# Row softmax with temperature on one core: the code alignment directives of DVE and ACT moved from the head of the code to behind the fourth pass

## The chip, the cores and the metric

The kernel runs on one core of a Trainium2 chip. The metric is the time of one execution on the device, in microseconds (us), as the median of several runs. All runs quoted here were at a granted clock of 1.0. A "ring" below is one of the core's 16 DMA engines, seen as a serial worker: it moves one packet after the other (in the trace of the kernel before, from 60 to 280 us, all but one of the 2,909 data packets start within 8 ns of the end of another packet). The packet records do not name the ring; what is said below of single rings is worked out from the times at which packets start and end.

## The reference

```python
def setup_inputs():
    batch, seq, dim = 32, 512, 1024
    return {"x": np.random.randn(batch, seq, dim).astype(np.float32), "temperature": 0.5}

def reference(x, temperature):
    scaled = x / temperature
    shifted = scaled - np.max(scaled, axis=-1, keepdims=True)
    exp_x = np.exp(shifted)
    return (exp_x / np.sum(exp_x, axis=-1, keepdims=True)).astype(np.float32)
```

There are 16,384 rows of 1,024 floats: 67.11 MB are read once and 67.11 MB written once.

## The kernel before

The rows are cut into 16 tiles of 4 MiB (128 partitions with 8 rows each), with six buffers. A pass works on half a tile, four rows per partition; there are 32 passes. DVE takes the maxima and later scales by the reciprocal sums, ACT takes the exponentials and issues the stores, SP issues the loads.

```python
    with tc.manual_schedule():

        nc.vector.addr_align(128, offset=0, max_nops=0)
        nc.scalar.addr_align(128, offset=0, max_nops=0)
        for _ in range(BUFS):
            load()
        for g in range(len(groups) + 1):
            if g < len(groups):
                maximum(g)         # DVE: reduction, then bias
                exponential(g)     # ACT: four exponentials with sums
            if g > 0:
                divide(g - 1)      # DVE: reciprocal, then four scalings
                store(g - 1)       # ACT: after each second pass; then load() on SP
```

The two directives ask that an engine's next instruction stand at a multiple of 128 slots of its code. The trace shows one branch for each, of 33 ns on ACT (at 0.73 us) and 47 ns on DVE (at 0.76 us).

Of the kernel before, what the change touches and what calls it, by code (L numbers as in the profile page):

```python
# [1 line left out]

# [4 lines left out]



TILES = [[8]] * 16  # L10
BUFS = 6

GROUP = 4


@with_exitstack
def kernel(
    ctx: ExitStack,
    tc: tile.TileContext,
    x: bass.AP,  # L20
    temperature: bass.AP,
    out: bass.AP,
):
    nc = tc.nc
    f32 = mybir.dt.float32
    scale = 1.0 / float(temperature)
    extreme = mybir.AluOpType.max if scale > 0 else mybir.AluOpType.min

    P = 128
    xf = x.flatten_outer_dims()  # L30
    of = out.flatten_outer_dims()
    n, d = xf.shape
    assert sum(sum(ks) for ks in TILES) * P == n

    data = ctx.enter_context(tc.tile_pool(name="data", bufs=BUFS))
    stats = ctx.enter_context(tc.tile_pool(name="stats", bufs=4))


    groups, first, r = [], [], 0
    for i, ks in enumerate(TILES):  # L40
        first.append(r)
        r += sum(ks)
        a = 0
        for k in ks:
            for b in range(0, k, GROUP):
                m = min(GROUP, k - b)
                groups.append((i, a + b, m, (a, k) if b + m == k else None))
            a += k

    def dram(t, i):  # L50
        k = sum(TILES[i])
        block = t[P * first[i] : P * (first[i] + k), :]
        return block.rearrange("(p k) d -> p k d", p=P, k=k)

    tiles, small = [], []

    def load():
        i = len(tiles)
        if i < len(TILES):
            xt = data.tile([P, sum(TILES[i]), d], f32, name="xt")  # L60
            nc.sync.dma_start(out=xt, in_=dram(xf, i))
            tiles.append(xt)

    def maximum(g):
        i, a, k, _ = groups[g]
        top, bias, sums, recip = (
            stats.tile([P, k], f32, name=name) for name in ("top", "bias", "sums", "recip")
        )
        small.append((bias, sums, recip))
        nc.vector.tensor_reduce(  # L70
            out=top, in_=tiles[i][:, a : a + k, :], axis=mybir.AxisListType.X, op=extreme
        )
        nc.vector.tensor_scalar_mul(bias, in0=top, scalar1=-scale)  # L73

    def exponential(g):
        i, a, k, _ = groups[g]
        bias, sums, _ = small[g]
        for b in range(k):
            nc.scalar.activation(  # L79
                tiles[i][:, a + b, :],  # L80
                tiles[i][:, a + b, :],
                mybir.ActivationFunctionType.Exp,
                bias=bias[:, b : b + 1],
                scale=scale,
                accum_out=sums[:, b : b + 1],
            )

    def divide(g):
        i, a, k, _ = groups[g]
        _, sums, recip = small[g]  # L90
        nc.vector.reciprocal(recip, sums)  # L91
        for b in range(k):
            nc.vector.tensor_scalar_mul(  # L93
                tiles[i][:, a + b, :], in0=tiles[i][:, a + b, :], scalar1=recip[:, b : b + 1]
            )

    def store(g):
        i, _, _, part = groups[g]
        if part:
            a, k = part  # L100
            nc.scalar.dma_start(out=dram(of, i)[:, a : a + k, :], in_=tiles[i][:, a : a + k, :])
            if a + k == sum(TILES[i]):
                load()



    with tc.manual_schedule():

        nc.vector.addr_align(128, offset=0, max_nops=0)
        nc.scalar.addr_align(128, offset=0, max_nops=0)  # L110
        for _ in range(BUFS):
            load()
        for g in range(len(groups) + 1):
            if g < len(groups):
                maximum(g)
                exponential(g)
            if g > 0:
                divide(g - 1)
                store(g - 1)


# [1 line left out]
_INS = ['x', 'temperature']  # L123
_OUTS = [((32, 512, 1024), 'float32')]

_NUMBERS = {'temperature': 0.5}


# [26 lines left out]
```

## Time and profile before

| | before |
|---|---|
| time, median of 3 runs | 317.72 us (317.58 to 317.98) |
| span of the profiled execution | 315.6 us |
| busy: DVE, ACT | 75%, 47% |
| bytes moved, mean rate | 134.26 MB, 425 GB/s |
| one 32 KiB data packet on its ring (median) | 1.213 us |
| start of the first DMA packet, end of the last | 1.74 us, 314.47 us |
| code packets (8,192 B each) start at | 1.76, 3.60, 124.63, 162.34, 253.33 us |

The last three rows come from the trace's records of single DMA packets; the views of the profile only sum them up.

### The profile page before, as it was taken

Reading aid. Unit: us, or ns where it says so; the run is one execution under the profiler, and the core shown is the slowest. Engines: PE = TensorE matmul, PEld = TensorE weight load, DVE = VectorE, ACT = ScalarE, POOL = GpSimd, SP = SyncE. Lnnn points to the kernel's source line nnn. Section 1 sums busy time; section 2 is a strip of 40 time slices with the busy share of each in tenths; the row PEclk is TensorE's granted clock in tenths of the full one; section 3 lists DMA queues with packets and bytes.
Section 4 is the critical chain, followed back from the end, with each engine's and each line's share of the span. In section 5 each row is a group of like instructions: output and inputs, shape, how many; then the busy total and the mean of one; then the engine's idle time right before and its main releaser. Section 6 shows DMA issues by size and latency. Waiting matters only on the chain.

```text
span 315.6 us, 622 instructions
## 1 busy us (share of the span) xinstructions
DVE 235.5 (75%) x224; ACT 149.6 (47%) x257; POOL 0.2 (0%) x4
## 2 busy tenths in 40 slices
DVE  0299999999789494994939949498594976949720
ACT  0176666666626255361553615546065560645500
POOL 0000000000000000000000000000000000000000
DMA  8999999999999999999999999999999999999996
GB/s 330 415 448 415 386 457 407 461 411 453 424 440 432 432 432 429 444 424 453 415 454 407 457 407 457 403 461 403 461 403 461 403 462 403 461 419 444 428 436 278
DMA packets 4613, 134.26 MB, mean 425 GB/s; under 512 B 512, under 2 KB 512, under 8 KB 512
## 3 DMA queue, kind: packets, MB, share of 16 engines
q1 hardware_dynamic: 2304, 67.11, 49.7%
q10 hardware_dynamic: 2304, 67.11, 49.2%
q14 instruction: 5, 0.04, 0.0%
HBM read 67.11 MB, written 67.11 MB: 425 GB/s over the span
## 4 chain that ended last, share of the span: by engine, by line
DVE 72%; another core or an unknown queue 15%; DMA 4%; ACT 3%; issue 1%; DVEq 0%
DVE top L70 43%; DVE xt L93 27%; DMA xt<-in_x_dram 4%; ACT xt L79 3%; DVE recip L91 1%; DVE bias L73 1%; DVEq L150 0%
## 5 line engine op out<-in xcount | busy, mean ns | idle before, releaser
L79 ACT ACTIVATE xt<-xt,bias 128x1024 f32<-128x1024 f32 x128 | 145.4, 1137 | 136.0 <-DVE recip L91 118.6
L70 DVE TENSOR_REDUCE top<-xt 128x4 f32<-128x4096 f32 x32 | 141.3, 4416 | 62.2 <-DMA xt<-in_x_dram 62.2
L93 DVE TENSOR_SCALAR xt<-xt,recip 128x1024 f32<-128x1024 f32 x128 | 87.7, 749 | 1.1
L79 ACT ACTIVATION_READ_ACCUMULATOR xt<-xt,bias 128x1 f32 x128 | 23.8, 186 | 0.0
L79 ACT ACT_TABLE_LOAD x1 | 1.3, 1283 | 13.5 <-DMA xt<-in_x_dram 13.5
L91 DVE RECIPROCAL recip<-sums 128x4 f32<-128x4 f32 x32 | 5.5, 171 | 2.1 <-ACT xt L79 2.1
L73 DVE TENSOR_SCALAR bias<-top 128x4 f32<-128x4 f32 x32 | 5.5, 170 | 1.1
L136 POOL MEMSET const-bfloat16-1.0<- 128x1 bf16 x1 | 0.1, 102 | 0.0
L136 POOL MEMSET const-uint8-127<- 128x1 uint8 x1 | 0.1, 102 | 0.0
L136 POOL MEMSET const-float32-0.0<- 128x1 f32 x1 | 0.1, 99 | 0.2 <-issue 0.2
L136 POOL MEMSET const-float32-1.0<- 128x1 f32 x1 | 0.1, 99 | 0.0
## 6 DMA issues: line engine op xcount, KB each, us to landing
xt<-in_x_dram SPq DMA_DIRECT2D x16, 4096.0 KB, 50.2
out_dram<-xt ACTq DMA_DIRECT2D x16, 4096.0 KB, 38.4
```

The source lines that it names most:

```text
L70: nc.vector.tensor_reduce(out=top, in_=tiles[i][:, a : a + k, :], axis=mybir.AxisListType.X, op=extreme)
L73: nc.vector.tensor_scalar_mul(bias, in0=top, scalar1=-scale)
L79: nc.scalar.activation(tiles[i][:, a + b, :], tiles[i][:, a + b, :], mybir.ActivationFunctionType.Exp, bias=bias[:, b : b + 1], scale=scal ...
L91: nc.vector.reciprocal(recip, sums)
L93: nc.vector.tensor_scalar_mul(tiles[i][:, a + b, :], in0=tiles[i][:, a + b, :], scalar1=recip[:, b : b + 1])
L136: nc = _bacc.Bacc("TRN2", target_bir_lowering=False, num_devices=1)
```

## The change

The intent: the padding and its branch stand in the middle of the work of the second tile, not ahead of everything. Nothing else moves: the order of instructions on each engine, the loads, the stores and the waits are the same.

```diff
+ALIGNED = 3
...
     with tc.manual_schedule():
-
-        nc.vector.addr_align(128, offset=0, max_nops=0)
-        nc.scalar.addr_align(128, offset=0, max_nops=0)
         for _ in range(BUFS):
             load()
...
                 divide(g - 1)
                 store(g - 1)
+            if g == ALIGNED:
+
+                nc.vector.addr_align(128, offset=0, max_nops=0)
+                nc.scalar.addr_align(128, offset=0, max_nops=0)
```

## The prediction

Passages of the text are cut, and the cuts are marked. The sum came to 0 (head) + 0 (branches hidden) + 0 (five fetches then, five now) = 0, so 317.7 us, the time before.

> **What bounds the kernel now.** I read the page first (its slices and its queues), then the waits of the DMA-issuing engine, then the chain that ended last and the timeline around the fourth pass and around the end. The page's slices and queues come first, because the reference is a row softmax over 64 MB that goes in and out once.
>
> ```profile
> span 315.6 us, 622 instructions
> ...
> DMA  8999999999999999999999999999999999999996
> GB/s 330 415 448 415 386 457 407 461 411 453 424 440 432 432 432 429 444 424 453 415 454 407 457 407 457 403 461 403 461 403 461 403 462 403 461 419 444 428 436 278
> ...
> q1 hardware_dynamic: 2304, 67.11, 49.7%
> q10 hardware_dynamic: 2304, 67.11, 49.2%
> q14 instruction: 5, 0.04, 0.0%
> HBM read 67.11 MB, written 67.11 MB: 425 GB/s over the span
> ```
>
> The DMA row is 9 (90% or more) in every slice but the first and the last; no engine row is (DVE is 75% busy in all, ACT 47%). So the 16 DMA engines bound it. The packets say how tightly: the median 32 KiB packet takes 1.213 us in the trace, and 16 x 32,768 B / 1.213 us = 432 GB/s. When I spread each packet's bytes evenly over its own time, nearly every 10 us stretch moves 433 GB/s, whatever mix of loads and stores is in it. The 134.22 MB at 433 GB/s are 309.8 us. The first packet starts at 1.73 us and the last ends at 314.47 us, 312.7 us later, so only 2.9 us are lost in the whole run: 0.9 us while the rings fill (before 5 us), 0.8 us around 35 to 38 us when the first store comes in, and the rest mostly because the rings do not all end together (the last packets of the final store end between 313.05 and 314.47 us).
>
> The q14 row is the one that the change concerns: five instruction packets, 0.04 MB. In the trace each is 8,192 B and takes 0.31 to 0.58 us on one of 16 rings; they start at 1.76, 3.60, 124.63, 162.34 and 253.33 us.
>
> The second view is the waits of the DMA queue's own engine, the third the chain of waits in order of time: start, length, what.
>
> ```profile
> SPq L61 <- DMA out_dram<-xt: 224.7, 10, 53.6
> SPq L150 <- DMA out_dram<-xt: 82.4, 5, 39.0
> ```
>
> ```profile
> 37.73 2.74 DVE xt L93 x4
> 40.47 4.34 DVE top L70
> 44.83 0.17 DVE bias L73
> ...
> 47.86 4.34 DVE top L70
> ...
> 84.80 3.14 another core or an unknown queue
> ...
> 102.83 4.47 another core or an unknown queue
> ```
>
> ```profile
> 299.02 0.19 DVE recip L91
> 299.24 0.75 DVE xt L93
> ```
>
> SP waits for stores to land, and from 84.8 us on DVE waits about 4.5 us in each tile for a load to land: that is what the "unknown queue" pieces are, since the waits view gives 62.2 us of DVE's idle time before L70 to the load. The chain's 72% on DVE should not mislead: DVE works without a pause from 22.8 to 84.8 us, but at 433 GB/s of traffic it is not what sets the pace. The page shows the same in group 5:
>
> ```profile
> L70 DVE TENSOR_REDUCE top<-xt 128x4 f32<-128x4096 f32 x32 | 141.3, 4416 | 62.2 <-DMA xt<-in_x_dram 62.2
> ```
>
> [...] the two directives of before appear as branches of 47 ns (DVE) and 33 ns (ACT), at 0.76 and 0.73 us. [...] the branches end by 0.80 us, and the second fetch starts at 3.60 us, 2.8 us later. [...]
>
> **The change part by part.** The order of instructions on both engines is the same before and after, save for the one directive each; I compared them. No load, store, tile or semaphore wait of the data path moves.
>
> Removed: two branches at the head, 47 + 33 ns. Both engines then wait for the first load until 13.4 us, so this is worth 0. With the branches go the fetches at 1.76 and 3.60 us: 0.58 + 0.33 = 0.91 us of two rings. The first load may land up to 0.6 us sooner, which shifts DVE's start; but those fetches are moved, not saved, so the rings' sum stays.
>
> Added on DVE: a branch between the fourth pass's scaling and the fifth reduction, at 40.4 us (the 37.73 and 40.47 rows). If the target block is already there, which is what I expect [...], it costs 0.05 us, under the running 0.75 us instruction. Added on ACT: a branch after the exponentials of the fourth pass, which end at 42.1 us; ACT's next starts at 45.09 us, so it has near 3 us of idle time, and its sequencer reaches the place even earlier (its next wait starts at 37.7 us).
>
> Moved: the later block borders. There were two borders of DVE in the span (head, and 162 us) and three of ACT (head, 125, 253 us). DVE's later border moves by the 23 instructions that now stand ahead of the directive in the trace's count, ACT's by 29. I expect five fetches again: two at 38 to 44 us, then near 156 us (ACT), 199 us (DVE) and 284 us (ACT). The borders of before show no gap: ACT's exponentials run 1.13 us apart straight through 119.4 to 124.1 us.
>
> The sum on the path that sets the end: -0 (head) + 0 (branches hidden) + 0 (five fetches then, five now; one more or fewer would be 0.3 us of one ring) = 0. So 317.7 us, the time before.
>
> **The rivals.**
>
> A. The branch finds its block missing and waits for it. A fetch under load takes about 2.8 us to start and 0.3 us to run (the second fetch at the head), so DVE would stand some 3 us at 40.4 us, and as it has no pause until 84.8 us, the stores at 47.9, 62.7 and 77.4 us would be issued 3 us later. Does that reach the end? By 40.4 us six loads and one store are queued, 7 x 4.194 = 29.4 MB, and some 16.0 MB have moved; the other 13.4 MB keep the rings full for 31 us, to about 71 us, while the next store comes at 47.9 us. So a stall under some 23 us leaves the rings full. Delayed stores only give the loads a larger share, they land sooner, and DVE takes the 3 us back from its waits of 3.1 us at 84.8 and 4.5 us at 102.8. Effect on the time: 0 to 0.5 us. [...]
>
> B. A wait in the tail. The last store is issued at 302.0 us and the store before it holds the rings until 304.8 us by its last packets, so the tail has about 2.8 us of slack. If ACT's last border (near 284 us) cost a demand fetch of 3.1 us there, DVE's last scaling would start about 3 us late and use the slack up: 0 to 0.5 us longer. Against: borders of before cost no gap.
>
> C. The rings' spread. The end waits for the slowest ring, and the rings end 1.42 us apart. Where the five fetches fall decides a part of that: 0.3 us for each on the slowest ring. This can go either way by about 0.3 to 0.9 us, and it alone could make the kernel faster.
>
> D. The change of rhythm: a store issued earlier or later changes how the loads and stores interleave. All mixes in the table of 10 us stretches run at 431 to 433 GB/s except the one with the first store (398), so I give it no more than half a microsecond.
>
> **Range and chances.** The expectation is 317.7. The three runs of before lie within 0.4 us; C gives about 0.6 us either way; A and B add up to 0.5 us each on the slow side with chances of about a quarter and a tenth. That makes 316.9 to 318.8 for 8 in 10. Two per cent is 6.4 us: to gain it, the rate would have to pass 440 GB/s[...]; to lose it, a stall of over 23 us at 40 us, or of about 9 us in the tail (the 2.8 us of slack plus 6.4), would be needed. I give faster 0.5%, within 2% 98%, slower 1.5%.
>
> **What would show it right or wrong.** Right: the DMA row 9 in all slices but the ends; five instruction packets of 8 KiB, two of them at 38 to 44 us; the fifth L70 (now two lines lower) right behind the scaling before it; the pauses of about 4.5 us in each tile and the last store's issue at 302 us within a microsecond. For A: DVE idle some 3 us before the fifth reduction, with seven or more packets, and shorter pauses at 84.8 us. For B: a hole in ACT or DVE after 280 us and a later last store. The prediction is wrong if the slices show the DMA engines below 9 anywhere in the middle, if a stall lasts tens of microseconds, or if the rings end with a spread much beyond 1.4 us.

## The result, and the profile after

The changed kernel takes 318.3 us (318.01 to 318.57, 6 runs), before 317.7 us (317.5 to 317.98, 6 runs). The ratio is 1.0018, with a 95% interval of 1.0005 to 1.0031. The ratios here and below are those of the record, for fast runs; they are not quite the ratios of the medians. The change costs about 0.2%: small, inside the predicted range, and on the slow side of zero.

The page of the changed kernel, its span, DMA slices and queues:

```profile
span 316.6 us, 622 instructions
...
DMA  8999999999999999999999999999999999999996
...
q1 hardware_dynamic: 2304, 67.11, 49.6%
q10 hardware_dynamic: 2304, 67.11, 49.1%
q14 instruction: 5, 0.04, 0.0%
HBM read 67.11 MB, written 67.11 MB: 424 GB/s over the span
```

The DMA engines are as full as before, there are again five code packets, and the span is 1.0 us longer. The timeline of DVE around the branch (start, length, engine, line, operation; several of a kind merged):

```profile
37.29 2.74 DVE L95 TENSOR_SCALAR xt<-xt,recip 128x1024 f32<-128x1024 f32 x4
39.95 4.41 DVE L72 TENSOR_REDUCE top<-xt 128x4 f32<-128x4096 f32 x1
```

The branch stands between these two groups, and the reduction starts as soon as it can behind the scalings; the second row even overlaps the first by 0.08 us, as such rows do before (22.96 + 2.74 against 25.61 us). So no engine stands still at the branch. The trace has the two branches at 37.24 us (ACT, 33 ns) and 37.31 us (DVE, 47 ns), ahead of the work still queued on the engines.

The pauses of DVE, in the chain of waits of the changed kernel, and its group of reductions:

```profile
84.35 3.70 another core or an unknown queue
102.94 4.68 another core or an unknown queue
```

```profile
L72 DVE TENSOR_REDUCE top<-xt 128x4 f32<-128x4096 f32 x32 | 141.3, 4414 | 63.2 <-DMA xt<-in_x_dram 63.2
```

DVE waits for loads as before, 63.2 us in place of 62.2. The extra microsecond is in waiting for data, not in work. The last scalings and the issue of the last store, first before, then after:

```profile
299.24 2.74 DVE L93 TENSOR_SCALAR xt<-xt,recip 128x1024 f32<-128x1024 f32 x4
302.01 0.34 ACTq L101 DMA_DIRECT2D out_dram<-xt  x1
```

```profile
300.23 2.74 DVE L95 TENSOR_SCALAR xt<-xt,recip 128x1024 f32<-128x1024 f32 x4
303.00 0.34 ACTq L103 DMA_DIRECT2D out_dram<-xt  x1
```

The tail is shifted by 0.99 us as a whole. What shifts it is seen in the packets, ring by ring. Each of the 32 transfers ends with one 4-byte packet on each of the 16 rings (the page counts 512 packets under 512 B). The table has, for the store before the last, by how much the slower rings end later than the fastest one (worked out from the trace's packet records):

```
                     fastest ring   how much later the five slowest end   last packet of all
before  store 15         303.37 us   0.27 0.47 1.29 1.36 1.42                    314.47 us
after   store 15         303.34 us   0.18 0.44 0.66 2.10 2.42                    315.44 us
```

The fast rings are where they were. Two rings are late by 2.10 and 2.42 us, where the slowest was late by 1.42 us. DVE begins with a load behind the slowest ring of it: that ring of the last load ends at 281.79 us before and at 282.76 us after, and DVE begins with its data 0.46 and 0.49 us later. For each of the twelve loads that DVE waits for in either trace it is 0.35 to 0.52 us, though the fastest ring is done up to 2.63 us ahead of the slowest. The execution ends behind the slowest ring of the last store, in both traces 1.2 us after its last packet: the 0.97 us between 314.47 and 315.44 us is nearly the whole difference of these two spans, 1.00 us. The two profiled executions lie further apart than the medians of all runs (0.6 us).

The code packets of the changed kernel start at 40.92, 43.18, 158.12, 201.72 and 279.69 us. The slow rings' lags grow in steps at just these times. Between the load whose fastest ring lands at 144.8 us and the one at 164.2 us, for instance, the largest lag goes from 1.25 to 1.78 us. A code packet takes 0.31 us, and the data packet beside it takes longer than the median of 1.213 us: by 0.25, 0.53, 0.24, 0.53 and 0.33 us at the five places. So each costs its ring 0.55 to 0.84 us. Before, the packets at 124.63, 162.34 and 253.33 us cost 0.42, 0.84 and 0.57 us by the same reckoning, but the two at the head fell into the time when the rings were filling.

### The profile page after: what moved, and what is told of

It is laid out like the page before. It is cut to its first block, busy times and chain, and to the rows that moved or that the text cites. A ratio compares the mean times of both kernels' runs of the same rounds, so it can differ in the third digit from the quotient of the medians.

```text
span 316.6 us, 622 instructions
## 1 busy us (share of the span) xinstructions
DVE 235.4 (74%) x224; ACT 149.6 (47%) x257; POOL 0.2 (0%) x4
## 4 chain that ended last, share of the span: by engine, by line
DVE 72%; another core or an unknown queue 16%; DMA 4%; ACT 3%; issue 1%; DVEq 0%
DVE top L72 43%; DVE xt L95 26%; DMA xt<-in_x_dram 4%; ACT xt L81 3%; DVE recip L93 1%; DVE bias L75 1%; DVEq L153 0%
## 5 line engine op out<-in xcount | busy, mean ns | idle before, releaser
L72 DVE TENSOR_REDUCE top<-xt 128x4 f32<-128x4096 f32 x32 | 141.3, 4414 | 63.2 <-DMA xt<-in_x_dram 63.2
```

The source lines that it names most:

```text
L72: nc.vector.tensor_reduce(out=top, in_=tiles[i][:, a : a + k, :], axis=mybir.AxisListType.X, op=extreme)
```

## The experiments

The theory after reading the traces, called S below, is this: a fetch of code delays only the ring that carries it, all fetches of one engine use one ring, and the execution ends with the slowest ring. The rivals: the branch itself costs time; the costs of all fetches add up; a fetch costs no more than its bytes; the difference is only how the rings happen to fill at the start.

All edits are against the kernel before; `v` stands for `nc.vector`, `s` for `nc.scalar`, and `align(n)` for `addr_align(n, offset=0, max_nops=0)`. All runs gave correct results. The first four ran on one chip with 5 rounds (before there: 317.69 us median of 11 runs, 317.52 to 317.99 but for one run of 319.48), the next four with 3 rounds (before: 317.75 us, 317.44 to 317.99), the last two with 3 rounds (before: 317.79 us, 317.47 to 318.56).

| run | what | median us | over before | code packets after 5 us | last packet, slowest ring | span |
|---|---|---|---|---|---|---|
| e1_late_again | both late (the change) | 318.13 | +0.44 | 5 | 315.07 | 316.3 |
| e2_none | no directive | 318.06 | +0.37 | 4, and one at the end | 315.12 | 316.3 |
| e3_dve_late | DVE's late | 318.13 | +0.44 | 4 | 315.62 | 316.8 |
| e4_act_late | ACT's late | 317.85 | +0.16 | 4 | 314.96 | 316.1 |
| e5_act_many | seven more on ACT | 320.93 | +3.18 | 8 | 318.06 | 319.2 |
| e6_dve_many | seven more on DVE | 323.47 | +5.72 | 9 | 320.31 | 321.5 |
| e7_both_many | seven more on both | 323.88 | +6.13 | 14 | 320.82 | 322.0 |
| e8_dve_hops | five on DVE within 1 us of work | 323.01 | +5.26 | 8 | 319.97 | 321.1 |
| e9_act_branches | seven on ACT, to 4 slots | 317.72 | -0.07 | 3 | 314.84 | 316.0 |
| e10_sp_many | seven on SP | 321.12 | +3.33 | 9 | 317.93 | 319.2 |

The last two columns stay 1.1 to 1.3 us apart in all ten: the span follows the slowest ring. At its limit of 2% the record classes e6, e7 and e8 as "unclear" and the others as "same"; the intervals given below say whether a difference is clear of zero.

### The four placements

The changed kernel again:

> The changed kernel once more, beside the next three on one chip. Theory S (slowest ring): an 8 KiB code fetch delays only the one DMA ring that carries it, by its own 0.31 us and by the 0.1 to 0.54 us that the data packet beside it takes longer; all fetches of one engine use one ring; the kernel ends when the slowest ring ends. Then: 318.3 us, +0.5 to +0.7 over before, two rings about 2 us behind the others in the last stores. Theory L (launch noise: the 0.6 us come from how the rings happen to fill at the start): the difference is anywhere between -0.3 and +0.7 and the lag of the slow rings differs from the first profile.

It is slower again, by 0.44 us in the medians. Its ratio of 1.0010 has an interval of 0.9992 to 1.0027, widened by the one run of before at 319.48 us, so these five rounds alone do not prove it. All twelve runs of the changed kernel, on two occasions, lie at 317.96 us or above; of the 31 runs of before, 29 lie at 317.99 or below. The two slowest rings are 2.03 and 1.65 us behind in the last stores, less than in the first profile: a part of the 2.42 us there was the start of that one execution. Theory L is right that far.

No directive at all:

```diff
-        nc.vector.addr_align(128, offset=0, max_nops=0)
-        nc.scalar.addr_align(128, offset=0, max_nops=0)
```

> No directive at all, so no branch and no padding; block borders fall where the code happens to lie. Theory S: what counts is how many fetches fall after 5 us on the busier of the two engines' rings; I expect two on ACT and one or two on DVE, so 317.3 to 317.9 us, within 0.4 us of before; each fetch in the trace shows as a step of 0.4 to 0.9 us in one ring's lag. Theory B (the branch itself costs something in the changed kernel): clearly the fastest of all, 0.5 us or more under before.

It takes 318.06 us (ratio 1.0004, interval 0.9988 to 1.0020), a little above the range I gave. It is not the fastest, so the branch is not what costs. There is no branch in this kernel, and yet code packets come at 64.24, 64.96, 181.77 and 241.77 us, all under full load: the borders fall there of themselves. Its slowest ring ends the last stores 2.17 us behind, like the changed kernel's (2.03 to 2.42). This suggests what the directives at the head are good for in the kernel before: they bring the first fetch of each engine forward into the time when the rings fill. The difference of 0.37 us is not clear of the noise, so the times do not show it.

Only DVE's directive late, then only ACT's:

```diff
         s.align(128)                   # at the head, as before
-        v.align(128)
...
+            if g == ALIGNED:
+                v.align(128)
```

> Only DVE's directive is moved; ACT's stays at the head. Theory S: ACT's ring as before (lag about 1.4 us in the last stores), DVE's ring as in the changed kernel (lag about 2.1 us): +0.3 to +0.6 over before. If the costs of the two directives simply add up: half of the whole, and with the next run they sum to it.

```diff
         v.align(128)                   # at the head, as before
-        s.align(128)
...
+            if g == ALIGNED:
+                s.align(128)
```

> Only ACT's directive is moved. Theory S: ACT's ring is the slowest of the changed kernel (lag 2.4 us), so this alone gives nearly the whole loss, +0.5 to +0.8 over before, and this and the run with DVE's alone sum to more than the whole. If costs add up: about half of the whole, +0.3.

DVE's alone gives +0.44 us, as much as both; ACT's alone gives +0.16 us. I had expected ACT's to give nearly the whole: that is a miss, and the first profile had misled me. The intervals of both ratios (0.9988 to 1.0024 and 0.9982 to 1.0015) contain 1, so these two runs can't decide between "the larger counts" (0.44 against the 0.44 of both) and "the costs add up" (0.44 + 0.16 = 0.60). The slowest two rings end the last stores 2.43 and 1.70 us behind with DVE's late, and 1.95 and 1.67 us with ACT's late. The trace with DVE's late shows the rings most clearly, since there all packets can be followed from end to start: fourteen rings carry 288 packets each, one carries 291, three of them the code packets at 1.79, 123.68 and 252.52 us (ACT's, by their places), and one carries 290, with those at 42.77 and 200.93 us (DVE's). The next runs make the effect larger.

### Many fetches on one engine, and on two

```diff
+            if g % 4 == 3 and g < 31:
+                s.align(128)           # e5; v.align(128) in e6; both in e7
```

> Both directives at the head, and seven more for ACT, after passes 3, 7, 11, ... 27 (the first is pass 0): ACT then enters a new block some 40 instructions after the last, seven fetches under load in place of two. Theory S: five fetches more on ACT's ring, 0.65 us each (mean of the six steps measured so far), so +3.2 us (2.2 to 4.2) over before, and the lag of one ring climbs in seven steps to 4 to 5 us. Rival (a fetch costs its bytes only, shared by all 16 rings): 5 x 8 KiB / 433 GB/s = 0.1 us, no difference.

> The same for DVE: seven fetches under load in place of one. Theory S: six more on DVE's ring, +3.9 us (2.6 to 5.0) over before. Rival: +0.1 us.

> Both sets together, eleven fetches more than before. Theory S with a ring for each engine: the rings lag side by side, so the larger of the two runs before, +3.9 us (not more than 0.5 us over it). If the costs of fetches add up whatever ring they take: the sum of the two, about +7 us. If fetches cost bytes only: +0.2 us.

The pages of the three runs, in this order, their span, DMA slices and code queue:

```profile
span 319.2 us, 629 instructions
...
DMA  8999999999999999999999999999999999999966
...
q14 instruction: 10, 0.08, 0.1%
```

```profile
span 321.5 us, 629 instructions
...
DMA  8999999999999999999999999999999999996966
...
q14 instruction: 11, 0.09, 0.1%
```

```profile
span 322.0 us, 636 instructions
...
q14 instruction: 16, 0.13, 0.1%
```

Five more code packets on ACT, 0.04 MB in 134 MB, cost 3.18 us (ratio 1.0103, interval 1.0088 to 1.0118), as expected. In this trace one ring alone falls back step by step, to 4.85 us in the thirteenth store, and each of the seven fetches under load costs it 0.31 us and 0.34 to 0.37 us of a slower data packet for all but the first (0.25): 0.66 us. The bytes alone would be 0.1 us by estimate (5 x 8 KiB at the 433 GB/s of the trace before), so the rival that counts bytes is out. In the DMA slices the last two fall to 6, where before it is the last alone, while the slowest ring works on until 318.06 us. The trace of the changed kernel shows such a fall in small: at 303.75 us, ahead of the last store, only 4 of the 16 rings are busy, and the slowest ring has no gap there of more than 3 ns.

On DVE the same costs 5.72 us (ratio 1.0190, interval 1.0170 to 1.0211), more than the range I gave. The packets say why. DVE's fetches slow the data packet beside them by 0.54 to 0.66 us, not by ACT's 0.35: with 0.31 us for the fetch itself about 0.95 us each, and 6 x 0.95 = 5.7 us. The number of additional fetches was right, my mean of both engines was the wrong size.

Both together cost 6.13 us (ratio 1.0198, interval 1.0183 to 1.0214): the larger of the two and 0.4 us, and not 3.18 + 5.72 = 8.9. Two rings fall back in this trace, to 7.85 and 5.70 us in the thirteenth store. So the costs of different engines lie side by side on different rings, and the slowest ring decides. This is the run that tells the maximum from the sum.

### Waiting for a block on purpose

```diff
     def divide(g):
         i, a, k, _ = groups[g]
         _, sums, recip = small[g]
+        hop(g)                         # v.align(128), only where g == 3
         nc.vector.reciprocal(recip, sums)
         for b in range(k):
+            hop(g)
             nc.vector.tensor_scalar_mul(
```

> Both directives at the head, and five more for DVE within one microsecond of work, before the reciprocal and each of the four scalings of the fourth division (near 45 us), so that each enters a block that cannot have arrived. This makes the stall of my rival A on purpose: four waits of about 3 us (2.8 us to start a fetch under load, 0.3 us to run), DVE idle for some 12 us between 45 and 65 us. If the backlog of the rings hides a stall of up to 23 us, as predicted: only the five extra fetches on DVE's ring count, +3.2 us (2.2 to 4.2) over before, DMA at 9 in all slices. If a stall of DVE reaches the end: +12 us or more.

The branch of each hop follows the instruction before it by about 20 ns (51.77 after 51.75 us, for instance). The timeline of DVE, with the idle time ahead of an instruction in brackets, and then the waits of this run and its DMA slices:

```profile
45.67 0.18 DVE L98 RECIPROCAL recip<-sums 128x4 f32<-128x4 f32 x1 [0.34 <-issue]
51.75 0.75 DVE L101 TENSOR_SCALAR xt<-xt,recip 128x1024 f32<-128x1024 f32 x1 [5.91 <-issue]
57.54 0.75 DVE L101 TENSOR_SCALAR xt<-xt,recip 128x1024 f32<-128x1024 f32 x1 [5.04 <-issue]
63.36 0.75 DVE L101 TENSOR_SCALAR xt<-xt,recip 128x1024 f32<-128x1024 f32 x1 [5.06 <-issue]
69.19 0.75 DVE L101 TENSOR_SCALAR xt<-xt,recip 128x1024 f32<-128x1024 f32 x1 [5.08 <-issue]
```

```profile
DVE xt L101 <- issue: 21.1, 4, 5.9
```

```profile
DMA  8999999999999999999999999999999999999990
```

A block that isn't there stops DVE for 5.0 to 5.9 us, not for 3, and four of them for 21.1 us. The packets show how: the code packet that a wait ends with starts 3.9 us after DVE went on in the block ahead (55.62 after 51.75 us, for instance; for the first wait it is 4.8 us after the branch at 45.17 us), takes 0.31 to 0.33 us, and DVE goes on 1.5 to 1.6 us after its end. "Issue" means that the profile shows nothing that DVE waits for: this is how such a stall looks. And still the DMA engines stay at 9 and the kernel loses 5.26 us (ratio 1.0179, interval 1.0154 to 1.0203), not 21. The five more fetches on DVE's ring account for most of it: 5 x 0.95 = 4.8 us, and the slowest ring lags 6.41 us in the last stores against 1.42 before, 5.0 us more. The kernel bore a stall of 21 us in the middle, as the prediction's estimate of the backlog let expect (some 23 us, to about 71 us). The stalls here end at 69.19 us, so this is one test just inside that estimate; where the limit lies is not shown. The range that I gave for the fetches was missed again by DVE's larger cost for each.

### The branch without the fetch, and the fetch on an engine that computes nothing

```diff
+            if g % 4 == 3 and g < 31:
+                s.align(4)             # e9; nc.sync.addr_align(128, ...) in e10
```

> The run with seven more ACT directives once more, but aligned to 4 slots in place of 128: ACT takes up to seven padding branches at the same places and stays in its block. Theory S (the fetch on the ring costs, not the branch): no new fetches, so as before within 0.3 us (317.5 to 318.1), five instruction packets, no steps in the ring's lag beside theirs. Rival (the branches, or padding that is run through, cost ACT time that reaches the end): +3 us, as in the run with 128 slots.

> Both directives at the head, and seven for the engine that only issues the loads, five of them between loads and two behind the last. It computes nothing, so nothing can wait for its work but the loads. Theory S with a ring for each engine: five to seven fetches under load on a third ring, 0.65 us (ACT's cost of one) to 0.95 us (DVE's) each, which begins about 0.3 us behind; it passes the slowest ring of before (1.4 us): +2 to +5 us. Rival (fetches matter only where a computing engine is held): within 0.3 us of before.

Aligned to 4 slots, ACT takes five branches under load (at the other two of the seven places the trace has none, presumably since the code was aligned there), but the page has the five code packets of before, and the time is that of before: 317.72 us (ratio 0.9995, interval 0.9978 to 1.0012).

```profile
span 316.0 us, 627 instructions
...
q14 instruction: 5, 0.04, 0.0%
```

So these five branches and their padding cost nothing that reaches the end (317.72 us against 317.79 before). Each of the seven directives on SP but the last, which had nothing in front of it, gives a branch and a fetch, six in all:

```profile
span 319.2 us, 628 instructions
...
DMA  8999999999999999999999999999999999999993
...
q14 instruction: 11, 0.09, 0.1%
```

They cost 3.33 us (ratio 1.0107, interval 1.0088 to 1.0125), though no computing engine is touched. One ring steps back to 4.85 us in the thirteenth store. Each fetch costs it 0.31 us and 0.41 to 0.42 us of a slower data packet (0.34 at the first): 0.71 us in the mean and 4.3 us for the six, from a ring that began about 0.35 us behind. The lag of 4.85 us less the 1.42 us of before is 3.4 us, near the 3.33 us measured. The cost is thus on the ring, on an engine that computes nothing (0.71 us each) as on ACT (0.66 us).

No version beat the kernel before clear of the noise. Little is to be had in this way: its slowest ring ends 1.42 us after its fastest, 0.4% of the time.

## Why the prediction was right or wrong

The number was right: 318.3 us measured, 317.7 expected, 316.9 to 318.8 the range, and no change beyond 2%. The expected change of zero was not: the interval of the ratio leaves it out. The range held because it left room for rival C. One of the prediction's own signs of being wrong did come, a spread of the rings "much beyond 1.4 us": 2.42 us in the store before the last and 1.85 us in the last.

**The bound** was right. The DMA engines stay at 9 in all inner slices in both kernels.

**The head.** That the two removed branches are worth nothing fits: DVE and ACT wait for the first load until 13.0 us in the changed kernel too, and the run with no directive is no faster. The sentence "those fetches are moved, not saved, so the rings' sum stays" is where the sum fails, with "+ 0 (five fetches then, five now; ...) = 0" after it. The count of five is right. But a fetch does not cost the same everywhere and not 0.3 us: under load it costs its ring about 0.66 us on ACT and 0.84 to 0.95 us on DVE, because the data packet beside it is slower too. ACT's fetch at the head, at 1.76 us, came about when its ring's first data came (the first data packets of the 16 rings start between 1.74 and 2.63 us). DVE's at 3.60 us is not free: the load that lands first has one ring 0.83 us behind and the next 0.34 us, so I estimate 0.5 us for it. Moving DVE's from an estimated 0.5 us to 0.84 us gives some 0.35 us on that ring. That is near the +0.44 us of DVE's directive alone; it explains the small loss in size, but the runs do not resolve it better than that.

**The branches.** That they are hidden was right: the reduction follows without a gap (at 39.95 us, behind scalings that end at 40.03 us), where a block made to be missing stopped DVE for 5.0 to 5.9 us, so the block was there; and the run with padding branches alone is as fast as before (317.72 us against 317.79). The five times of the fetches (38 to 44 twice, 156, 199, 284 us) were right within 5 us: 40.92, 43.18, 158.12, 201.72, 279.69.

**Rival A** did not happen in the changed kernel. Made on purpose, its stall was 5.0 to 5.9 us for a block, where I had taken 3 us from the second fetch at the head: a fetch under load began after 3.9 to 4.8 us and not 2.8, and the 1.5 to 1.6 us from its end to the next instruction were missing from the sum. Its other half, that a stall under some 23 us leaves the rings full, held: 21.1 us of stall were absorbed but for the fetches' own cost.

**Rival B** did not happen: no new hole in ACT or DVE after 280 us. The last store comes 0.99 us later because the last load's slowest ring lands later (282.76 us against 281.79), and the fast rings then run dry for about half a microsecond (4 of 16 are busy at 303.75 us, all 16 at 304.0 us), which costs nothing, since the slow ring has no gap there of more than 3 ns.

**Rival C** was the mechanism: "0.3 us for each on the slowest ring". The size was off by a factor of two to three (0.66 us on ACT, 0.71 on SP, 0.84 to 0.95 on DVE). That all fetches of one engine pile up on one ring, so that they do add up there, I had not said. The enlarged runs show this mechanism; for the changed kernel itself only the lags of its rings and the estimate above speak for it.

**Rival D** is not seen: the stretches of the changed kernel run at 431 to 434 GB/s but for the one with the first store (403), the one around the start of the last (415), and the ends (320 and 167).

What stays open: how the 0.44 to 0.6 us divide between the two directives, since those runs differ by no more than their spread; and why a fetch for DVE slows the packet beside it more than one for ACT or SP.

## What to carry to other kernels

When the DMA is the bound, look at the slowest of its 16 engines, not at their mean: here five more code packets for ACT, 0.04 MB that all rode the same one, delayed the end by 3.18 us, where their bytes come to an estimated 0.1 us. Keep code blocks from being entered more often than needed while the DMA is full (each cost its ring 0.66 to 0.95 us in the runs with many), by short code and perhaps by a first border before the data starts (these runs do not show that part clear of the noise); and read a difference of half a microsecond from the records of the packets, because no view of the engines showed it here. A long backlog of queued transfers can hide a stall on a computing engine: here 21.1 us of DVE's waits left a loss of 5.26 us, of which the fetches alone are an estimated 4.8 us. So a stall that is seen is not yet a stall that costs.
